# Nested attention over ragged sequences: twice as many loop bodies, V projected by tiles, and a fetch-and-jump between bodies

## The chip, the cores and the metric

The kernel runs on one core of a Trainium2 chip. The metric is the device time of one execution in microseconds (us), given as the median over several executions. Most executions of one kernel agree within a few us. Each execution carries a state, "fast" or "slow"; comparisons below use fast runs only. A ratio is the mean time of one kernel's fast runs over the mean of the other kernel's fast runs of the same rounds on the same chip, so it is not quite the ratio of the medians that are quoted beside it: the medians are over all runs, among them one slow run each of the kernel after and of e1_layout.

Names of engines in the profile: PE is TensorE's matrix multiply, PEld its weight load, DVE is VectorE, ACT is ScalarE, POOL is GpSimd, SP is SyncE. A name with q at its end (PEq) is that engine's sequencer.

## The reference, cut to what matters

```python
batch, max_seq, n_heads, head_dim = (32, 512, 8, 64)
lengths = np.random.randint(64, max_seq, size=batch)

for b in range(batch):
    seq_len = lengths[b]
    qkv = np.matmul(x[b, :seq_len], w_qkv)          # 512 -> 3 * 512
    q, k, v = ...                                    # 8 heads of 64
    scores = scale * np.matmul(q, k.transpose(0, 2, 1))
    attn = softmax(scores)                           # with 1e-08 in the denominator
    output[b, :seq_len] = np.matmul(attn, v)         # the rest stays zero
```

There are 32 sequences with lengths between 64 and 511, known only at run time.

## The kernel before

The kernel ranks the sequences by length on the chip, longest first, and takes them two at a time: 16 pairs, called pair 0 to pair 15 here. Each pair has a class, its longer length rounded up to a multiple of 32. For each class there is one body: a fixed stream of instructions for every engine, which computes the attention of two sequences and meanwhile projects Q, K and V of the next one, so that TensorE always has something to do. A tile is 128 rows, so the body of class 352 is a "three-tile" body. The bodies stand in the program one after the other, from class 512 down to 64. Each engine walks down this list; a body whose class is not the current one is jumped over, and a body whose class comes again is repeated.

```python
CLASSES = [32 * k for k in range(16, 1, -1)]

ORDER = {   # S scores, Q K V projections, A attention times V, O P stores
    4: "S S Q0 A0 S S K0 V0 S S Q1 A1 S S K1 V1 S S Q2 A2 S S K2 V2 S S Q3 A3 S S K3 V3 O",
    3: "S S Q0 A0 K0 S S V0 Q1 A1 S S K1 V1 S S Q2 A2 K2 S S V2 Q3 A3 S S K3 V3 O",
    2: "S S V0 B0 A0 b1 A1 S V1 S B2 V2 O A2 A3 b3 P V3",
}
# ... cut ...
def read_class(pr, h, N):          # once in a body, in its first half
    if h == 0:
        for g in ("pe", "act", "dve"):
            pr.add(g, lambda e: next_class(e))       # class of the next pair -> register
        k = CLASSES.index(N)
        if k + 2 < len(CLASSES):
            def hint(e):
                cur, far = regs[e.engine][1], regs["far"]
                e.reg_alu(far, cur, k + 2, ALU.is_lt)
                ahead[k + 1] = e.mark_branch_hint_location(far)
            pr.add("pe", hint)
# ... cut ...
def loops(e, name, body, pre1=None):
    r, cur = regs[e.engine]
    for k, N in enumerate(CLASSES):
        if N == P and pre1 is not None:
            pre1(e)                                  # the "bridge" to one-tile bodies
        top = nc.cur_bb
        lab, out_ = f"{name}_b{k}", f"{name}_x{k}"
        br = e.br_cmp(cur, k, lab, out_, "IS_EQ")
        if name == "pe" and k in ahead:
            br.branch_hint(ahead[k])
        nc.switch_bb(lab, parent=top)
        body(e, N)
        e.br_cmp(cur, k, lab, out_, "IS_EQ")         # the same class again?
        nc.switch_bb(out_, parent=top)
```

V is projected by pairs of heads: for each of the T tiles, four matmuls with 128 columns.

```python
def vproj(pr, bank, h, i, T):
    # ... cut: T == 1 ...
    for t in range(T):
        for c in range(NC):
            mms.append(mm(
                pa[:, bank, t * P : (t + 1) * P],
                xT[h][:, c, t * P : (t + 1) * P],
                w_r[:, c, 2 * D + i * P : 2 * D + (i + 1) * P],
                c == 0, c == NC - 1,
            ))
    group(...)
```

The softmax here doesn't subtract the row's maximum and nothing guards it: scores larger than these inputs give would overflow.

## Time and profile before

| before | value | from |
|---|---|---|
| time, median | 370.14 us (368.4 to 371.85) | 3 runs |
| span in the profile | 367.7 us | page |
| PE busy | 349.1 us, 95% | page |
| mean granted TensorE clock | 0.986 | clocks by core |
| PE gaps over 0.9 us, summed | 3.3 us | trace |

The first fence has lines of the profile's page for the kernel before. The first gives each engine's busy time; the two strips give 40 equal slices of the span, each digit the busy tenths of PE or the granted clock in tenths; the last two are the queues that the page calls "instruction": packets, megabytes and their share of the DMA engines.

```profile
PE 349.1 (95%) x4844; PEld 245.4 (67%) x4845; DVE 236.9 (64%) x537; ACT 229.2 (62%) x307; POOL 58.0 (16%) x85
...
PE   8699999999999999999999999999899999999882
...
PEclk9699999999999999999999999999999999999998
...
q8 instruction: 32, 0.52, 0.6%
q14 instruction: 22, 0.18, 0.2%
```

PE is busy nearly always: TensorE bounds this kernel, and whatever takes PE's time away shows in the time.

The view of waits (engine, line, tile, what it waited for; total us, times, longest us) has for PE and PEld in the kernel before:

```profile
PEld pa L219 <- issue: 37.3, 121, 1.3
...
PEld psc L219 <- issue: 10.2, 31, 1.0
```

"issue" means that the engine waited for nothing that the profile can see. Weight loads have such waits between groups of matmuls all the time (152 in these two lines).

### The profile page before, as it was taken

What the parts mean: (1) busy time and instruction counts of PE and PEld (TensorE: products, weight loads), DVE (VectorE), ACT (ScalarE), POOL (GpSimd) and SP (SyncE); (2) the same over time, 40 slices, a digit from 0 to 9 for tenths busy, and PEclk for the clock granted to TensorE, in tenths of its full rate; (3) what the DMA queues carried; (4) which work ended last, traced back from release to release, by engine and by line L of the source; (5) the groups of instructions that cost most, each with busy time, mean ns of one, the idle gap of its engine ahead of it and who ended that gap; (6) DMA issues with size and microseconds to landing.
All of it is one profiled execution on the core that took longest, in us unless ns stands there. A gap on an engine that the chain in (4) does not pass through costs nothing. (4 is left out here: it accounts for less than half of the span.)

```text
span 367.7 us, 12708 instructions
## 1 busy us (share of the span) xinstructions
PE 349.1 (95%) x4844; PEld 245.4 (67%) x4845; DVE 236.9 (64%) x537; ACT 229.2 (62%) x307; POOL 58.0 (16%) x85
## 2 busy tenths in 40 slices
PE   8699999999999999999999999999899999999882
PEld 3245566666656666666666677777789898887761
DVE  4455667666767667676766767676666666676562
ACT  5278778777776666666666757565566664654541
POOL 3062020202010110111011001110112112212120
PEclk9699999999999999999999999999999999999998
DMA  7969677458759677978759759969876566667673
GB/s 264 337 155 276 202 160 215 132 123 265 182 168 237 172 257 192 225 260 289 225 150 302 252 117 286 299 199 255 233 203 184 152 176 182 188 143 223 164 169 101
DMA packets 84582, 76.43 MB, mean 208 GB/s; under 512 B 42544, under 2 KB 63024, under 8 KB 84528
## 3 DMA queue, kind: packets, MB, share of 16 engines
q1 hardware_dynamic: 69376, 59.47, 59.8%
q10 hardware_dynamic: 15152, 16.26, 12.9%
q8 instruction: 32, 0.52, 0.6%
q14 instruction: 22, 0.18, 0.2%
HBM read 29.37 MB, written 36.70 MB: 180 GB/s over the span
## 5 line engine op out<-in xcount | busy, mean ns | idle before, releaser
L261 ACT ACTIVATE ep<-psc 128x704 f16<-128x704 f32 (+5 forms) x265 | 204.7, 821 | 101.3 <-PE psc L219 76.6
L219 PE MATMUL pa<-xT,w_r 128*128 128x352 f16 (+11 forms) x1056 | 161.6, 288 | 3.8 <-PEq L45 2.6
L291 DVE CAST qkT<-pa 128x352 f16<-128x352 f32 (+5 forms) x164 | 92.0, 561 | 59.5 <-PE pa L219 55.5
L219 PEld LDWEIGHTS pa<-xT,w_r 128*128 128x128 f16 x1056 | 81.4, 98 | 54.4 <-issue 27.9
L219 PE MATMUL pa<-w_r,xT 128*128 128x128 f16 (+1 forms) x1296 | 94.8, 221 | 0.1
L219 PEld LDWEIGHTS pa<-w_r,xT 128*128 128x128 f16 x1296 | 77.8, 98 | 18.4 <-issue 9.4
L324 DVE TENSOR_TENSOR v_aug<-pa,masks 128x384 f16<-128x384 f32 (+2 forms) x116 | 60.9, 525 | 31.5 <-PE pa L219 29.7
L219 PEld LDWEIGHTS pav<-v_aug,ep 128*128 128x128 f16 x1792 | 67.2, 98 | 11.7 <-ACT ep L261 3.5
L219 PE MATMUL pav<-v_aug,ep 128*128 128x65 f16 x1792 | 71.7, 194 | 2.5 <-ACT ep L261 2.4
L219 PE MATMUL psc<-qkT 64*128 64x352 f16 (+11 forms) x656 | 70.1, 299 | 1.4 <-PEq L45 0.9
L405 DVE SCALAR_TENSOR_TENSOR onat<-pav,masks,rcp 128x256 f32<-128x256 f32 (+2 forms) x128 | 51.9, 444 | 5.2 <-DVE rcp L381 0.7
L849 POOL CAST v_aug<-masks 128x24 f16 (+4 forms) x33 | 9.1, 276 | 282.1 <-POOLq L665 282.1
L844 POOL CAST x<-x_nat 128x1536 f16<-128x1536 f32 (+3 forms) x34 | 43.9, 1293 | 17.2 <-POOLq L665 16.2
L219 PEld LDWEIGHTS psc<-qkT 64*128 64x128 f16 x656 | 20.6, 94 | 21.5 <-issue 10.2
L289 ACT CAST qkT<-pa 128x448 f16<-128x448 f32 (+3 forms) x28 | 14.1, 504 | 24.4 <-ACTq L45 15.2
L381 DVE RECIPROCAL rcp<-pav 128x8 f32<-128x8 f32 (+1 forms) x68 | 14.7, 216 | 19.7 <-PE pav L219 16.0
L403 DVE TENSOR_TENSOR onat<-pav,rcp 128x512 f32<-128x512 f32 (+2 forms) x32 | 17.8, 557 | 1.1
L883 PE MATMUL psc<-zt 128*128 128x512 f16 x26 | 7.9, 468 | 1.7 <-DVE zt L905 1.7
L883 PEld LDWEIGHTS psc<-zt 128*128 128x128 f16 x26 | 2.8, 114 | 5.2 <-issue 1.9
L610 ACT ACTIVATE ep<-tiny 128x1024 f32<-128x1024 f32 x6 | 6.0, 1053 | 0.0
L790 ACT CAST w_r<-w_f 128x1024 f16<-128x1024 f32 x4 | 4.2, 1045 | 1.1 <-DMA w_f<-in_w_qkv_dram 1.1
L790 ACT ACT_TABLE_LOAD x1 | 1.3, 1283 | 3.2 <-issue 3.2
(48 smaller groups left out, 19.7 us busy)
## 6 DMA issues: line engine op xcount, KB each, us to landing
out_dram<-zt SPq DMA_DIRECT2D x16, 768.0 KB, 5.4
x_nat<-in_x_dram SPq DMA_DIRECT2D x12, 768.0 KB, 5.0
x_nat<-in_x_dram SPq DMA_DIRECT2D x8, 1024.0 KB, 6.6
out_dram<-onat ACTq DMA_DIRECT2D x28, 256.0 KB, 3.5
x_nat<-in_x_dram SPq DMA_DIRECT2D x12, 512.0 KB, 4.2
out_dram<-onat ACTq DMA_DIRECT2D x12, 384.0 KB, 3.9
out_dram<-onat SPq DMA_DIRECT2D x12, 384.0 KB, 3.6
out_dram<-zt SPq DMA_DIRECT2D x12, 256.0 KB, 4.6
```

The lines of the kernel that those rows point to most:

```text
L219: return lambda e: e.matmul(o, lhsT, rhs, start=start, stop=stop)
L261: lambda e: e.activation(out=dst, in_=src, func=AF.Exp, scale=scale),
L289: group(pr, b, eng, mms, lambda e: e.copy(out=dst, in_=src))
L291: group(pr, b, eng, mms, lambda e: e.tensor_copy(out=dst, in_=src))
L324: lambda e: e.tensor_tensor(out=v_aug[h][:, 0:T, 2 * i : 2 * i + 2, 0:HD], in0=pa[:, bank, 0 : T * P].rearrange("p (t a d) -> p t a d", a= ...
L381: pr.add("dve", lambda e: e.reciprocal(out=rv, in_=den).then_inc(s_r, 1))
L403: ins = e.tensor_tensor(op=ALU.mult, **ops)
L405: ins = e.scalar_tensor_tensor(scalar=now[0][:, 1, t : t + 1], op0=ALU.mult, op1=ALU.mult, **ops)
L610: lambda e, a=a: e.activation(out=ep32[:, i + 1, a], func=AF.Copy, in_=tiny.unsqueeze(2).broadcast_to([P, NT, MAXS // 2]),).then_inc(s_ini ...
L844: e.tensor_copy(out=x16[h][:, 0:T, :], in_=x_nat[h][:, 0:T, :]).then_inc(s_xc[h], 1)
L849: e.tensor_copy(out=v_aug[h][:, 0:T, :, HD], in_=src[:, 0, 0:T].unsqueeze(2).broadcast_to([P, T, NH]),).then_inc(s_on[h], 1)
L883: e.matmul(psc[:, 1, 0, :], zt16[:, 0:P], zt16[:, 0:MAXS], start=True, stop=True)
```

## The change

The intent has four parts. (1) A pair's second sequence may be one class (32 columns) shorter than the first, with a body of its own: 29 bodies instead of 15 (in the numbering here, 0 to 28; 24 to 28 are one-tile bodies), each of which knows how many columns it really has to project. (2) In the prologue and in bodies of three and four tiles V is projected by tiles: one group of four matmuls with 512 columns per tile instead of groups of 128 columns. Bodies of two tiles keep V by pairs of heads. (3) In the middle of its first half, each body looks up the next class, and "fetches": it compares the class with the bodies within reach and marks, for the one that fits, a hint to the later jump there. (4) At its end, the body jumps straight to the next body instead of walking down the list. The token orders of the bodies change with it. The diff, cut to its core:

```diff
+DOWN = 1
+BODIES = [(k, k + d) for k in range(NCL) for d in range(DOWN + 1) if k + d < NCL]
+REACH = 4
...
+    def vproj(pr, bank, h, t):
+        mms = []
+        for c in range(NC):
+            mms.append(
+                mm(pa[:, bank, :], xT[h][:, c, t * P : (t + 1) * P], w_r[:, c, 2 * D : 3 * D],
+                   c == 0, c == NC - 1)
...
-        3: "S S Q0 A0 K0 S S V0 Q1 A1 S S K1 V1 S S Q2 A2 K2 S S V2 Q3 A3 S S K3 V3 O",
+        3: "S S Q0 A0 K0 S S V0 Q1 A1 S S K1 V1 S S Q2 A2 V2 S S K2 A3 S S Q3 K3 O",
...
+    def targets(at):
+        end = first1 if at < first1 else len(BODIES)
+        near = [to for to in range(max(at, 0), at + REACH + 1) if to < end]
+        return sorted(near, key=lambda to: (to != at + 1, to != at + 2))
...
+    def fetch(pr, at):
+        def fn(g, e):
+            ...
+            for to in targets(at):
+                skip = to == at + 1
+                if skip and g != "pe" or g != "pe" and at < to < at + 3:
+                    continue
+                e.br_cmp(cur, number(to), f"{name}{to}", f"{name}{to}n", "IS_EQ")
+                nc.switch_bb(f"{name}{to}", parent=top)
+                if not skip:
+                    pr.ahead[g][to] = e.mark_branch_hint_location()
+                e.br(f"{name}x")
+                nc.switch_bb(f"{name}{to}n", parent=top)
+            e.br(f"{name}x")
+            nc.switch_bb(f"{name}x", parent=top)
...
-    def loops(e, name, body, pre1=None):
+    def loops(e, name, body, pre1=None, before={}):
...
+        def leave(at, ahead):
+            for to in targets(at):
+                d = f"{name}_d{at}_{to}"
+                br = e.br_cmp(cur, number(to), f"{name}_b{to}", d, "IS_EQ")
+                if to in ahead:
+                    br.branch_hint(ahead[to])
+                nc.switch_bb(d, parent=top)
+            e.br(f"{name}_x{max(targets(at))}")
+
+        leave(-1, before)
+        nc.switch_bb(f"{name}_x-1", parent=top)
+        for at in range(len(BODIES)):
+            if at == first1 and pre1 is not None:
                 pre1(e)
-            top = nc.cur_bb
-            lab, out_ = f"{name}_b{k}", f"{name}_x{k}"
-            br = e.br_cmp(cur, k, lab, out_, "IS_EQ")
-            ...
+            lab, out_ = f"{name}_b{at}", f"{name}_x{at}"
+            e.br_cmp(cur, number(at), lab, out_, "IS_EQ")
             nc.switch_bb(lab, parent=top)
-            body(e, N)
-            e.br_cmp(cur, k, lab, out_, "IS_EQ")
+            leave(at, body(e, at) or {})
             nc.switch_bb(out_, parent=top)
```

TensorE marks no hint for the next body in the list (at + 1), on the ground that it comes next anyway. And a body is now two blocks of code with the fetch's little branches between them: a head and a tail.

With the lengths of this case the bodies run in the order 1, 4, 8, 10, 10, 11, 13, 14, 16, 18, 19, 21, 22, 23, then the bridge, then 25 and 26.

## The prediction

> **What bounds the kernel now.** TensorE. The page shows PE busy 349.1 of 367.7 us, and the timeline by engine shows its groups back to back from 30.7 to 344 us. The table of busy times by stretch gives, for a pair of three-tile sequences (133 to 158 us), PE 25.1 of 25.1 us, against DVE 17.2 and ACT 16.7. Exceptions: the start (Q and K begin at 14.4 us), the prologue's end (ACT runs unpaused from 20.9 to 32 us and sets when the first pair starts), ACT's wait for the zero fill (PE lost 1.06 us at 262), ACT late at the start of short bodies (PE lost 0.46 at 321, 0.90 at 334 us), and the last six us of stores.

> **Where the change can gain.** Sorted into classes, pairs 0, 5, 6, 10, 11, 13 and 14 of the 16 have a shorter second rank; they project, and score their second half, 32 columns narrower.

> 1. Narrower columns. By the timeline a column costs 0.42 ns (four matmuls of 512: 0.87 us, of 352: 0.61). In a pair of T tiles the projections lose 64 x 32 columns = 0.85 us, scores 0.13 (T=2) to 0.5 us (T=4). Estimates: pair 0 1.4, pairs 5 and 6 1.25 each, 10 and 11 1.0 each: 5.9 us.
> 2. Pair 13 goes from 160/160 to 160/128, so its second half becomes a one-tile half. It takes 15.2 us now with the bridge (331.2 to 346.4). I estimate 6.0 (with a stall of about 1.2 us at the fence, which waits for DVE's reciprocal and products) + 3.1 + 0.8 us, so 4 to 5 us less.
> 3. Pair 14 is one-tile; there the transposes (3.2 us to landing, PE gaps of 0.27 and 1.17 us) are about as long as a half, so I expect nearly nothing.
> 4. V by tiles. 896 matmuls of 128 columns become 224 of 512. But 16 of them take 0.99 us where four of 512 take 0.87 us, and 0.08 us of this belongs to the following scores (64-row weights) and stays. So 2 to 3 ns per matmul: about 0.04 us per group of 16, 2 us in all. [...] In three-tile halves A3 now comes only one K (0.61 us) after its last scores, while ACT needs 0.75 us: perhaps 0.15 us of stall in each of 12 halves, which takes it back.
> 5. Fetch and jump. [...] ACT's "issue" gaps of 1.5 and 2.3 us at starts of bodies agree. But PE lost only about 0.5 to 1.5 us to these. More distinct bodies run (15 instead of 12), compares are hidden. Net gain about 0.5 us.
> 6. Class calculation on DVE grows about 1.1 us, absorbed while x's third tile loads.

> **Sum:** 5.9 + 4.7 + about 1 = 11.6 us: 370.1 becomes 358.5 us, range 354 to 363.5. Chances: faster 0.84, same 0.13, slower 0.03.

> **What would show it:** V matmuls at 217 ns, V's PE time nearly unchanged; pair 13 with bridge near 10 us; pairs 1 to 4, 7 to 9 within 0.3 us of before.

> **What would make it wrong:** fetch stalls at +2 to +4 jumps on ACT, DVE, SP; DVE (two-tile halves now evacuate Q3 and K3 there) becoming the limit; the A3 stalls larger; prologue's V waiting for its weights (cast ends at 22.4 us).

ACT's gaps are in the trace of the kernel before: five waits of ACT marked "issue" at starts of bodies, 1.3 to 2.3 us, 8.2 us together.

## More of the kernel before

The 32 packets of q8 have 16384 bytes each, the 22 of q14 have 8192.

Finally, a piece of PE's timeline in pair 1 (start us, length us, engine, line, operation, shapes, count):

```profile
77.31 1.06 PE L219 MATMUL pa<-w_r,xT 128*128 128x128 f16 x16
78.30 0.55 PE L219 MATMUL psc<-qkT 64*128 64x448 f16 x4
78.78 0.93 PE L219 MATMUL pa<-xT,w_r 128*128 128x448 f16 x4
79.55 1.12 PE L219 MATMUL pav<-v_aug,ep 128*128 128x65 f16 x32
```

The groups follow each other without a bracket for idle time. `pa<-w_r,xT` is a V projection, `psc` scores, `pa<-xT,w_r` a Q or K projection, `pav` attention times V.

## The result, and the profile after

| | before | after |
|---|---|---|
| median | 369.97 us (368.4 to 371.85, 4 runs) | 442.86 us (439.38 to 446.49, 4 runs, one of them slow) |
| span in the profile | 367.7 us | 440.2 us |
| PE busy | 349.1 us | 364.4 us |
| span less PE busy | 18.6 us | 75.8 us |
| mean granted clock | 0.986 | 0.911 |
| PE gaps over 0.9 us, summed | 3.3 us | 58.9 us |

The ratio is 1.194 (95% interval 1.184 to 1.204): 19% slower, where 3% faster had been predicted. The same lines of the page as before, now of the kernel after:

```profile
PE 364.4 (83%) x4080; PEld 218.2 (50%) x4081; DVE 237.4 (54%) x526; ACT 217.1 (49%) x291; POOL 57.4 (13%) x85
...
PE   7779999699779668999899589696695995978582
...
PEclk9698999899889967999999979899898899799778
...
q8 instruction: 46, 0.75, 0.7%
q14 instruction: 47, 0.39, 0.3%
```

The total loss of span splits without a rest: 57.2 us more in which PE does nothing, and 15.3 us more of PE busy, though PE now runs 4080 matmuls instead of 4844 with fewer columns. The busy time grew because the clock fell, from a mean of 0.986 to 0.911. Nor did other engines get more to do: DVE is where it was, and ACT has less. Both instruction queues brought more: 46 packets instead of 32, and 47 instead of 22.

The waits of the kernel after:

```profile
PEld pa L227 <- issue: 77.4, 148, 5.3
...
PEld psc L227 <- issue: 55.9, 81, 4.2
...
PE pa L227 <- issue: 26.2, 8, 4.9
PE psc L227 <- issue: 24.0, 9, 3.9
```

The last two lines are 17 waits of PE of the kind "issue", 50.2 us in total. In them it isn't waiting for DVE, ACT or a transfer of data, as far as the profile shows. Their place in the timeline is the first real clue. This is pair 1 again:

```profile
79.35 0.93 PE L227 MATMUL pa<-xT,w_r 128*128 128x448 f16 x4
83.86 1.03 PE L227 MATMUL pa<-w_r,xT 128*128 128x512 f16 x4 [3.58 <-issue]
```

and pairs 2, 3 and 8, and the end of pair 7:

```profile
126.47 1.89 PE L227 MATMUL pa<-w_r,xT 128*128 128x512 f16 x4 [2.56 <-issue]
...
166.79 1.46 PE L227 MATMUL pa<-w_r,xT 128*128 128x512 f16 x3 [4.93 <-issue]
...
307.55 1.04 PE L227 MATMUL psc<-qkT 64*128 64x256 f16 x8 [3.29 <-issue]
...
317.65 1.04 PE L227 MATMUL pa<-w_r,xT 128*128 128x128 f16 x8 [3.35 <-issue]
```

There are two places where PE stops. Seven times it stops in the middle of a body, each time at its fetch point (2.56 to 4.93 us, 24.8 us together: pairs 1, 2, 3, 6, 8, 9, 11). Eight times it stops at the entry of a pair, as at 307.55 us (2.11 to 3.92 us, 22.9 us together: pairs 0, 2, 3, 5, 6, 7, 8, 12). One gap of 4.23 us follows the bridge, and five of 1.1 to 1.6 us (one of them before the first projection) are of other kinds. Sum 58.9 us.

During one of those mid-body gaps, from 80.2 to 83.9 us, the view of DMA queues shows:

```profile
q1 hardware_dynamic: 896, 0.21, 41.5%
q8 instruction: 2, 0.03, 3.6%
```

Two packets of q8 start in it, the first at 80.34 us, 0.06 us after PE's last matmul ended. In each of the seven mid-body gaps a packet on q8 starts between 0.4 us before the gap and 1.8 us after its beginning, takes 0.9 to 2.3 us, and PE resumes only after it has landed. A packet alone stops nothing: 32 came on q8 in the kernel before, whose large gaps sum to 3.3 us, and none of the 32 starts inside one of these gaps.

The clock's part shows in the table of busy times by stretch (stretch, length, then busy us of PE, PEld, DVE, ACT, POOL, then the granted clock, the DMA share and GB/s), just after the entry gap of pair 2 and the mid-body gap of the same pair:

```profile
116.00:119.40 3.40, 3.21 (x27) 1.86 (x28) 0.56 (x1) 1.51 (x2) 1.76 (x2) 0.50 0.35 116
126.30:129.70 3.40, 3.23 (x11) 0.88 (x12) 0.75 (x1) 0.86 (x2) 0.00 (x0) 0.50 1.02 378
129.70:133.00 3.30, 3.30 (x41) 1.69 (x40) 1.51 (x3) 1.77 (x3) 0.00 (x0) 1.00 0.32 122
```

After most of the gaps, PE runs for 3.4 to 10.2 us at half clock (granted 0.50), so that such a gap costs more than its own length: the four matmuls at 126.47 us took 1.89 us, the same group at 83.86 us, still at full clock, 1.03 us. The kernel after has 15 half-clock stretches, the kernel before has 2, one near the start and one at the end. Of the 16 gaps over 2 us in the list above, 13 came with a half-clock stretch; those of pairs 5, 6 and 12 (2.11, 2.46 and 3.05 us at the entry) did not, so the length of a gap alone does not tell. The gaps of 2.56 and 2.60 us of pair 2 came with 3.4 us at 0.50 each, the one of 3.05 us with none.

### Where the code stands

The compiled instruction stream of TensorE explains the places. It was read from the built program (no view of the profile shows it), with the number of the first and last matmul slot of each part of a body:

```
kernel after, TensorE
body  1:  head 1092 to 1294   tail 1309 to 1945
body  4:  tail 3686 to 4322   head 4331 to 4533
body  8:  tail 6986 to 7414   head 7423 to 7561
body 10:  tail 8166 to 8594   head 8603 to 8741
```

Bodies 0 to 3 stand as they were written. From body 4 on, up to the last two-tile body, the blocks were laid out with the tail before its own head. The cause in the source is the chain of fall-back labels x0, x1, ...: `leave` ends with a jump to x{max(targets)}, a label that earlier bodies so refer to, and the layout of blocks puts x{at-1} and the head after it behind the tail. (That the labels are the cause is shown by the first experiment below, which does away with them and gets the written order.) So with its own fetch point each such body jumps back, to its tail: by about 850 instructions in body 4, 575 in bodies 8 and 10, 465 in most two-tile bodies and 280 in the last one; and from the end of the tail it jumps over its own head and over the next tail to the next head. "The next body needs no hint, it comes next anyway" was no longer true.

At each of the fifteen gaps of the two kinds a packet of 16384 bytes on q8 starts between 0.5 us before the gap and 1.8 us after its beginning. (That q8 is TensorE's is inferred: PE resumed in the mid-body gaps only after such a packet had landed, and the runs e8_pefetch and e9_allhint, which change the fetch of ACT and DVE alone, moved q14, from the 47 packets of e6_align to 44 and 49, and left q8 at 40. Which engines q14 serves, the trace does not say.) A part that ran again did not always bring packets: body 10 ran a second time in pair 4, and no packet on q8 starts after 163.69 us and before 214.12 us, at that pair's end. The stall was 2.1 to 4.9 us, the transfer of the packet itself 0.9 to 2.3 us.

The pattern of the mid-body gaps fits this layout to the last body. All seven rotated bodies that were entered by a jump of +2 or more (4, 8, 10, 13, 16, 18, 21) stopped in their middle. Of the six passes that began by a jump of +1 or in the same body (10 again, 11, 14, 19, 22, 23), none did: there the tail had just run or lies just behind what ran before; why PE did not stop there is not shown. Three of those five +1 entries (11, 14, 22) stopped at the entry instead (2.11, 3.92 and 3.05 us), where the head lies behind the tail and no hint was given. The entries with a hint are not explained: the trace has nine hint records of TensorE, for the entries of pairs 0 to 4, 6, 8, 9 and 11, and those of pairs 0, 2, 3, 6 and 8 stopped all the same.

### The profile page after: what moved, and what is told of

Same layout as the page of the kernel before. It is cut to its first block, busy times and chain, and to the rows that moved or that the text cites. A ratio compares the mean times of both kernels' runs of the same rounds, so it can differ in the third digit from the quotient of the medians.

```text
span 440.2 us, 11342 instructions
## 1 busy us (share of the span) xinstructions
PE 364.4 (83%) x4080; PEld 218.2 (50%) x4081; DVE 237.4 (54%) x526; ACT 217.1 (49%) x291; POOL 57.4 (13%) x85
## 5 line engine op out<-in xcount | busy, mean ns | idle before, releaser
L269 ACT ACTIVATE ep<-psc 128x704 f16<-128x704 f32 (+6 forms) x261 | 197.7, 807 | 193.8 <-PE psc L227 157.9
L227 PE MATMUL pa<-xT,w_r 128*128 128x96 f16 (+12 forms) x1056 | 159.6, 294 | 8.4 <-PEq L51 6.0
L299 DVE CAST qkT<-pa 128x352 f16<-128x352 f32 (+6 forms) x172 | 93.6, 549 | 74.7 <-PE pa L227 73.1
L227 PE MATMUL pa<-w_r,xT 128*128 128x128 f16 (+1 forms) x568 | 97.0, 311 | 26.7 <-issue 24.7
L227 PE MATMUL psc<-qkT 64*128 64x352 f16 (+12 forms) x644 | 69.8, 310 | 25.2 <-issue 24.0
L227 PE MATMUL pav<-v_aug,ep 128*128 128x65 f16 x1768 | 76.2, 200 | 4.6 <-issue 1.6
L227 PEld LDWEIGHTS pav<-v_aug,ep 128*128 128x128 f16 x1768 | 70.7, 102 | 17.6 <-issue 7.0
L311 DVE TENSOR_SCALAR v_aug<-pa,masks 128x512 f16<-128x512 f32 x62 | 46.6, 752 | 60.3 <-PE pa L227 55.5
L227 PEld LDWEIGHTS pa<-w_r,xT 128*128 128x128 f16 x568 | 43.0, 105 | 59.3 <-issue 39.4
L902 POOL CAST x<-x_nat 128x1536 f16<-128x1536 f32 (+3 forms) x34 | 43.1, 1268 | 15.6 <-POOLq L720 15.1
L334 DVE TENSOR_TENSOR v_aug<-pa,masks 128x256 f16<-128x256 f32 x40 | 16.9, 422 | 24.2 <-PE pa L227 24.0
L391 DVE RECIPROCAL rcp<-pav 128x8 f32<-128x8 f32 (+1 forms) x67 | 14.4, 215 | 24.4 <-PE pav L227 19.5
L297 ACT CAST qkT<-pa 128x384 f16<-128x384 f32 (+3 forms) x16 | 8.0, 500 | 15.9 <-ACTq L51 12.4
```

The costliest lines, as they stand in the source:

```text
L227: return lambda e: e.matmul(o, lhsT, rhs, start=start, stop=stop)
L269: lambda e: e.activation(out=dst, in_=src, func=AF.Exp, scale=scale),
L297: group(pr, b, eng, mms, lambda e: e.copy(out=dst, in_=src))
L299: group(pr, b, eng, mms, lambda e: e.tensor_copy(out=dst, in_=src))
L311: lambda e: e.tensor_scalar(out=v_aug[h][:, t, :, 0:HD], in0=pa[:, bank].rearrange("p (h d) -> p h d", d=HD), scalar1=now[0][:, 0, t : t + ...
L334: lambda e: e.tensor_tensor(out=v_aug[h][:, 0:T, 2 * i : 2 * i + 2, 0:HD], in0=pa[:, bank, 0 : T * P].rearrange("p (t a d) -> p t a d", a= ...
```

## The experiments

The theory: most of the loss is the place of the code, heads behind tails, and what jumps over them cost; the computation that the change wanted is nearly as good as predicted. The rivals: the fetch point costs by itself (its compares, the hints); V by tiles and the new order leave PE short of ready work; more bodies and narrower columns need other bodies more often, wherever they stand. Nine kernels ran; all gave the right result. The kernel before ran in the same rounds with medians of 370.57 us (e1 to e4), 370.48 us (e5 to e7) and 369.48 us (e8, e9).

All spans and gaps below are from the profiled run:

| run | median us | ratio to before, 95% interval | span | PE busy | clock | PE gaps over 0.9 us |
|---|---|---|---|---|---|---|
| after | 442.86 | 1.194 (1.184 to 1.204) | 440.2 | 364.4 | 0.911 | 58.9 |
| e1_layout | 383.13 | 1.037 (1.032 to 1.043) | 378.2 | 345.5 | 0.970 | 17.4 |
| e2_nofetch | 402.08 | 1.084 (1.082 to 1.087) | 403.3 | 352.7 | 0.940 | 36.6 |
| e3_vtiles | 372.10 | 1.004 (1.002 to 1.006) | 370.7 | 350.7 | 0.981 | 4.0 |
| e4_down0 | 371.87 | 1.002 (0.998 to 1.006) | 371.3 | 350.2 | 0.983 | 7.5 |
| e5_down0_rot | 395.80 | 1.065 (1.059 to 1.071) | 395.7 | 360.2 | 0.957 | 23.2 |
| e6_align | 367.32 | 0.991 (0.986 to 0.997) | 365.9 | 339.6 | 0.982 | 9.3 |
| e7_best | 367.34 | 0.989 (0.983 to 0.995) | 366.1 | 338.8 | 0.983 | 10.5 |
| e8_pefetch | 367.67 | 0.994 (0.988 to 1.000) | 365.1 | 340.1 | 0.981 | 7.5 |
| e9_allhint | 369.48 | 0.998 (0.990 to 1.005) | 368.1 | 338.7 | 0.988 | 11.1 |

### e1_layout: the same bodies, head directly before tail

The fall-back labels between bodies are replaced by one block before the one-tile bodies and one at the end. In the kernel after, the entry checks at these labels were run only on the fall-back path, so all but a few of the executed instructions are the same: the same 4080 matmuls in the same order.

```diff
-        def leave(at, ahead):
+        def leave(at, ahead, tos=None, other=None):
-            for to in targets(at):
+            for to in tos or targets(at):
...
-            e.br(f"{name}_x{max(targets(at))}")
+            e.br(other or f"{name}_{'one' if at < first1 else 'end'}")
...
-            if at == first1 and pre1 is not None:
-                pre1(e)
-            lab, out_ = f"{name}_b{at}", f"{name}_x{at}"
-            e.br_cmp(cur, number(at), lab, out_, "IS_EQ")
-            nc.switch_bb(lab, parent=top)
+            if at == first1:
+                nc.switch_bb(f"{name}_one", parent=top)
+                if pre1 is not None:
+                    pre1(e)
+                leave("one", {}, list(range(first1, len(BODIES))), f"{name}_end")
+            nc.switch_bb(f"{name}_b{at}", parent=top)
             leave(at, body(e, at) or {})
```

> The kernel after, with the same blocks and the same instructions in them, but the entry checks and skip labels between bodies removed, so that the toolchain lays the blocks out as written: each body's first part (up to the fetch) directly before its second part. In the kernel after, from the fifth body on, the second part lies before the first, so PE jumps some 650 to 850 instructions back in the middle of a body. Theory 'placement': the 7 gaps in the middle of bodies (24.7 us of PE waiting on issue) go, and the gaps at the entry of the bodies that follow directly (pairs 5, 7, 12: 9.1 us) go; some of those after jumps over a body stay; with the clock restored I expect 370 to 388 us. Rival 'fetch code': the compares, taken branches and hints themselves, or twice the code, cost the time wherever they lie: 425 us or more. Rival 'order of the work': V by tiles and the new orders cost it: no change, about 442 us.

Measured: 383.13 us, 60 us less than after. In the built program every tail follows its head. Pair 1's timeline at the place where the kernel after stopped for 3.58 us, and the waits:

```profile
78.08 0.93 PE L227 MATMUL pa<-xT,w_r 128*128 128x448 f16 x4
78.91 1.03 PE L227 MATMUL pa<-w_r,xT 128*128 128x512 f16 x4
```

```profile
PEld pa L227 <- issue: 37.5, 113, 2.8
PEld psc L227 <- issue: 35.6, 78, 4.1
...
PE psc L227 <- issue: 7.0, 2, 3.9
```

None of the seven mid-body gaps is left. Against after, the span fell by 62.0 us: 43.1 us of idle PE and 18.9 us of PE busy, which is the clock (0.911 to 0.970). That is 86% of the whole loss of 72.5 us. By the medians the fall is 59.7 us; the profiled run of e1_layout was its fastest. So the place of the code is the main cause, shown by changing almost nothing else. (The edit moves the blocks of every engine, since all use the same `loops`; that the stops were TensorE's own is read from its waits and branch records.) It isn't the whole: the kernel is still 3.7% slower than before, with 17.4 us of large gaps, among them 3.13 us after the prologue, 3.87 us at the entry of pair 11 and 2.68 us early in pair 14.

### e2_nofetch: good places, but no fetch point

As e1_layout, and `fetch` does nothing:

```diff
-        pr.ahead = {}
+        pr.ahead = {g: {} for g in ("pe", "act", "dve")}
+        return
```

> As e1_layout, and the fetch (compares and branch hints inside the bodies) taken out on all engines; only the jumps at the ends stay. If hints help: PE stalls about 3.5 us at each of some 9 jumps over a body, so 10 to 25 us slower than e1_layout (390 to 405 us). If the fetch code itself is the cost: faster than e1_layout.

Measured: 402.08 us, 19 us more than e1_layout. PE stops at the entry of eight of the 14 pairs before the bridge, for 2.3 to 5.5 us each, which is this line of its waits:

```profile
PE psc L227 <- issue: 29.0, 8, 5.5
```

So the fetch point is not the cost; with heads and tails in order it saves 19 us by the medians. (The profiled spans, 403.3 against 378.2 us, differ by 25 us, but they are of the slowest run of e2_nofetch and the fastest of e1_layout.) The rival "the fetch costs by itself" is out.

### e3_vtiles: the kernel before, with V by tiles and the new orders

```diff
+        if T >= 3:
+            for c in range(NC):
+                mms.append(
+                    mm(pa[:, bank, :], xT[h][:, c, i * P : (i + 1) * P], w_r[:, c, 2 * D : 3 * D],
+                       c == 0, c == NC - 1)
+                )
+            group(...)
+            return
...
-        3: "S S Q0 A0 K0 S S V0 Q1 A1 S S K1 V1 S S Q2 A2 K2 S S V2 Q3 A3 S S K3 V3 O",
+        3: "S S Q0 A0 K0 S S V0 Q1 A1 S S K1 V1 S S Q2 A2 V2 S S K2 A3 S S Q3 K3 O",
```

(the four-tile order and the prologue's order changed likewise)

> The kernel before with only V by tiles (three and four tiles), and the orders of work for them and for the prologue, from the kernel after. My prediction: V itself gains 2 us, the third A's stall takes some back: 368 to 371 us. Rival 'order of the work' (this part is what made the kernel after slow): over 400 us.

Measured: 372.1 us, ratio 1.004. Three-tile pairs without a class change take 25.83 to 25.93 us instead of 25.62 to 25.66: 0.2 to 0.3 us more each. V by tiles is next to neutral, a little worse, and cannot explain 72 us. The forecast, 368 to 371 us, was missed by 1 us. The profiled run also has a stop that isn't V's, at the entry of pair 2, where the list jumps over a class. The timeline of PE there:

```profile
107.07 0.60 PE L219 MATMUL psc<-qkT 64*128 64x384 f16 x4 [2.38 <-issue]
```

### e4_down0: good places, one body for each class again

As e1_layout with `DOWN = 0`: no shorter second rank, 15 bodies.

```diff
-DOWN = 1
+DOWN = 0
```

> As e1_layout with DOWN = 0: one body per class, both ranks of a pair at the first one's class, so no narrower projections. Against e1_layout this takes out the gain that I estimated at 10 to 11 us from narrower columns and pair 13, and takes out half of the bodies, so fewer jumps over a body (4 instead of 9, at about 2.5 us each). Expected 372 to 385 us; if narrowing gains what I said and jumps cost what I said, within 5 us of e1_layout.

Measured: 371.87 us, ratio 1.002. With the bodies in order, fetch and jump over 15 bodies is as good as the list of before, no better: the prediction's gain of 0.5 us for it is within the noise. The second half of the expectation, within 5 us of e1_layout, was missed: e1_layout took 11 us more in the same rounds. So the third rival is true in part: even in good places, 29 bodies at first cost more in jumps than their narrower columns gained (large PE gaps of 17.4 us in e1_layout, 7.5 in e4_down0).

### e5_down0_rot: the kernel after with one body for each class

The kernel after with `DOWN = 0` alone, so its tails stand before their heads. Against e4_down0, only the placement differs.

> The kernel after with DOWN = 0 and nothing else: one body per class, as e4_down0, but with the jump labels of the kernel after, so that from the fifth body on the second part again lies before the first. If placement is the cause, this is slow with the old number of bodies too: 8 bodies (pairs 2, 3, 6 to 11 and 12) run for the first time in that form, each with about 3.5 us in its middle and 2 to 3.5 us at its entry, and the clock lost after it: 415 to 440 us. If the doubled code is needed for the loss: within 10 us of e4_down0 (371.9 us).

Measured: 395.8 us, 24 us more than e4_down0 (in other rounds; the ratios to before are 1.065 and 1.002): the placement costs without any change of the work. The size was a miss: 415 to 440 us had been expected. Here is the same place of pair 2 in e5_down0_rot, and then in e4_down0:

```profile
110.00 0.82 PE L227 MATMUL pa<-xT,w_r 128*128 128x384 f16 x4
113.23 1.04 PE L227 MATMUL pa<-w_r,xT 128*128 128x512 f16 x2 [2.41 <-issue]
```

```profile
110.34 0.82 PE L227 MATMUL pa<-xT,w_r 128*128 128x384 f16 x4
111.00 1.03 PE L227 MATMUL pa<-w_r,xT 128*128 128x512 f16 x4
```

This is the only mid-body gap in e5_down0_rot. The others are five entry gaps of 2.25 to 3.41 us (pairs 3, 6, 7, 8, 9). With 15 bodies only one rotated body is entered by a jump of more than one, body 4 in pair 2, and this is the one that stops in its middle; the five entry gaps are all jumps of +1 (two more, into pairs 11 and 12, did not stop). For the gap inside a body it is the pattern of the kernel after, and it fits that fewer bodies lost less: with twice the bodies, seven of the 13 jumps between pairs 0 and 13 became +2 or more, and many bodies stopped at their entry and in their middle.

### e6_align: e1_layout, with heads placed at fixed offsets

This kernel pads TensorE's stream so that heads start 64 instructions (three and four tiles), 0 (others) or 100 (the last two-tile body) after a multiple of 256, aligns the prologue as well, and gives the bodies after the bridge hints from the last two-tile body.

```diff
+    HEAD = [64 if CLASSES[k] > 2 * P else 0 for k, _ in BODIES]
+    HEAD[first1 - 1] = 100
...
+            tos = targets(at)
+            if at == first1 - 1 and g == "pe":
+                tos = tos + list(range(first1, len(BODIES)))
...
+        pr.add("pe", lambda e: e.addr_align(256, offset=176, max_nops=0))
...
+            if name == "pe" and nxt < len(BODIES) and at != first1 - 1:
+                e.addr_align(256, offset=(HEAD[nxt] - 1) % 256, max_nops=0)
```

> As e1_layout, and on PE alone: padding that is never run puts the head of each body at a fixed place[...], the prologue is moved[...], and the chain of compares after the bridge gets hints. Theory: the remaining gaps of e1_layout at jumps (3.1 us after the prologue, 2.3 into pair 2, 3.9 into pair 11, 0.8 + 2.7 in pair 14) come from hinted blocks fetched too late[...]. Then they shrink by 8 to 12 us together, and with the clock: 366 to 374 us. If hints don't work that way: within 3 us of e1_layout (383 us).

Measured: 367.32 us, ratio 0.991 (0.986 to 0.997): faster than before, by a little under 1%. The gap after the prologue fell from 3.13 to 0.97 us, and pair 14, the first after the bridge, from 10.75 to 7.60 us. The entry of pair 11, first in e1_layout, then in e6_align:

```profile
309.62 0.82 PE L227 MATMUL pa<-xT,w_r 128*128 128x192 f16 x8
314.31 0.70 PE L227 MATMUL psc<-qkT 64*128 64x192 f16 x8 [3.87 <-issue]
```

```profile
304.42 0.82 PE L227 MATMUL pa<-xT,w_r 128*128 128x192 f16 x8
305.17 0.51 PE L227 MATMUL psc<-qkT 64*128 64x192 f16 x8
```

Three things changed together and the offsets were chosen for this path of bodies, so which of them did this is not shown, nor a rule for when a hint helps. One large gap stayed, 2.31 us at the beginning of pair 2, the jump from body 4 to body 8. The timelines of ACT, DVE and PE have there:

```profile
107.84 2.92 ACT L269 ACTIVATE ep<-psc 128x768 f16<-128x768 f32 x4 [3.80 <-issue]
...
107.96 1.02 DVE L299 CAST qkT<-pa 128x384 f16<-128x384 f32 x2 [3.19 <-issue]
...
108.71 0.34 PE L227 MATMUL psc<-qkT 64*128 64x384 f16 x2 [2.31 <-ACT ep L269]
```

PE waits for ACT here, and ACT and DVE wait for nothing visible, right after their jump. With TensorE mended, other engines' jumps come to light.

### e7_best: e6_align, with V by pairs of heads in three-tile bodies

```diff
-        3: "S S Q0 A0 K0 S S V0 Q1 A1 S S K1 V1 S S Q2 A2 V2 S S K2 A3 S S Q3 K3 O",
+        3: "S S Q0 A0 K0 S S W0 Q1 A1 S S K1 W1 S S Q2 A2 K2 S S W2 Q3 A3 S S K3 W3 O",
```

(W is V by pairs of heads; three-tile heads then start at offset 0)

> As e6_align, with V of three-tile halves by pairs of heads in the order of the kernel before (T2 tiles). The traces of e1_layout and e3_vtiles show three-tile pairs at 25.8 to 25.9 us against 25.6 before, so 0.2 to 0.35 us per pair come back: 1 to 2 us less than e6_align; 364 to 372 us, and perhaps faster than the kernel before (370.6).

Measured: 367.34 us, ratio 0.989. Pairs 3 to 7 take 0.1 to 0.5 us less than in e6_align, pair 2 takes 1.7 us less and pair 8 takes 3.1 us more in the profiled run, so the whole is not to be told from e6_align. The intervals of both lie just below 1.

### e8_pefetch and e9_allhint: ACT's and DVE's own fetch

Both are e6_align with TensorE's part untouched. e8_pefetch takes the fetch point from ACT and DVE; e9_allhint lets them mark hints for +2 and for the same body as well.

```diff
 e8:
-        for g in ("pe", "act", "dve"):
-            pr.add(g, lambda e, g=g: fn(g, e))
+        pr.ahead = {g: {} for g in ("act", "dve")}
+        pr.add("pe", lambda e: fn("pe", e))
 e9:
-                if skip and g != "pe" or g != "pe" and at < to < at + 3:
+                if skip and g != "pe":
```

> Same as e6_align, but ACT and DVE have no fetch point in the middle of a body any more (no compares, no hints); only TensorE keeps it. In e6_align TensorE still loses 2.3 us at the first two bodies of pair 2, because ACT is idle for 3.80 us and DVE for 3.19 us marked issue at that +4 jump although both had fetched. Theory A (ACT's and DVE's fetch helps the +3 and +4 jumps, only not enough at pair 2): without it pairs 1, 2, 3 and 10 lose 0.5 to 3 us each, 369 to 374 us. Theory B (the fetch on ACT and DVE [...] is the reason of the 3.8 us): the gap in pair 2 shrinks to below 1 us, 364 to 366 us. Matmul stream unchanged in both.

> Same as e6_align, but ACT and DVE also fetch ahead for a jump of +2 and for staying in the same body (before: only for +3 and +4). Theory A (a hint that is missing costs something at +2 jumps): small gaps at entries of pairs 3, 5, 10 to 12 that ACT ends shrink by 0.2 to 1 us each, 364 to 367 us; the +4 jump of pair 2 stays at 2.3 us. Theory B[...]: nothing or a shift of a gap from one pair to another, 366 to 370 us.

Measured: 367.67 and 369.48 us; the intervals of both overlap that of e6_align and include 1. Without its fetch, ACT's gap at pair 2 shrank from 3.80 to 2.32 us and pair 2 from 31.29 to 29.79 us; no other pair grew by more than 0.3 us (the prologue, by 0.7 us). So the fetch on ACT and DVE brings nothing measurable here, and part of the stall at pair 2 comes with it (theory B of e8, but only in part: PE still stops there twice, 0.83 and 1.44 us). With hints for +2, pair 1 became 1.6 us longer, with a new gap of ACT of 2.44 us, and none of the pairs named (3, 5, 10 to 12) got shorter: as theory B of e9 expected (366 to 370 us), for a reason that is not shown. What would clear pair 2 fully stays open.

## Why the prediction was wrong

The prediction was 358.5 us (354 to 363.5); the measured time was 442.86 us. The step that failed is item 5, "More distinct bodies run (15 instead of 12), compares are hidden. Net gain about 0.5 us". It was costed by the number of compares and by stalls that ACT had shown before. Where the compiler would put the two halves of each body was not asked; the prediction took the order of the source for the order in memory. What the runs showed in its place:

- The placement cost 62.0 us of span in the profiled runs (after against e1_layout; 59.7 us by the medians): 43.1 us of idle PE and 18.9 us through the lower clock. The second term was not in the prediction at all.
- With the placement mended, something that e6_align removed still cost about 12 us: e1_layout to e6_align, 378.2 to 365.9 us of span (15.8 us by the medians, in different rounds). It shows at jumps of TensorE: the gap after the prologue fell from 3.13 to 0.97 us, the entry of pair 11 from 3.87 us to none, and pair 14 after the bridge took 7.60 us instead of 10.75; since e6_align changed three things at once, the share of each is not shown.
- Of what could make it wrong, the prediction named "fetch stalls at +2 to +4 jumps on ACT, DVE, SP". It had a stall, but the wrong engines and only the jumps between bodies: the stalls were TensorE's own, and about half of them lay inside a body, at the jump from head to tail that the written order does not have. ACT and DVE show one in e6_align, pair 2, of 2.3 us for PE.

The other items can be read where the placement doesn't hide them, from a body's first scores to the next body's:

| item | predicted gain | measured |
|---|---|---|
| 1 narrower columns, pairs 0, 5, 6, 10, 11 | 5.9 us | 3.6 us: 1.2, 1.0, 0.7, 1.1, and -0.4 in pair 11 (e4_down0 to e6_align) |
| 2 pair 13 with the bridge | 4 to 5 us (15.2 to about 10) | 2.9 us (15.2 in before, 12.3 in e6_align) |
| 3 pair 14 | nearly nothing | 0.5 us longer than before (e6_align) |
| 4 V by tiles | a wash | 0.2 to 0.3 us lost per three-tile pair (e3_vtiles) |
| 5 fetch and jump | 0.5 us | in before's set of bodies 0 (e4_down0); in the kernel after a loss of about 60 us by the placement alone |

Item 1 was right in mechanism; its sizes for pairs 6 and 11 were too high. Item 2's stall at the fence was predicted as about 1.2 us and measured as 1.27 us; but the bridge grew by 0.5 us (0.73 to 1.23), and pair 13 without the bridge took 11.1 us where 6.0 + 3.1 = 9.1 us had been estimated. Pair 2 is the item that was missing from the sum: 27.16 us before, 31.29 in e6_align. The order of tokens is not the reason: e4_down0 has the same order, jumps by two bodies there, and takes 26.84 us. (The 28.42 us of e3_vtiles include its stop of 2.38 us.) That leaves the jump from body 4 to body 8, at which ACT and DVE stand still (3.80 and 3.19 us). Pair by pair, from before to e6_align, the sum is -1.8 us, of which pair 13 without the bridge gives -3.4, pair 0 -1.7, pairs 5, 6 and 10 together -2.1, and pair 2 takes back 4.1.

Item 4 had also named V's duration: the group of four 512-column matmuls takes 1.03 us in the listings above (they start 215 to 217 ns apart, as predicted), the 16 of 128 columns 1.06 us (mostly 56 ns apart, in the kernel before). That was right, and so was the lack of a gain.

## What to carry to other kernels

When a kernel has many bodies and jumps between them, read the compiled order of its blocks before anything else: labels that are referred to from earlier code can turn a body inside out, and here a part that was not laid out in the order of execution cost 2 to 5 us wherever TensorE stopped for it, and in 12 of 15 cases some us at half clock beside it. In the profile, look for PE waits marked "issue" of over 2 us with a packet on the instruction queue beside them; they belong to no data and no engine as far as the profile shows, and an average of busy time doesn't name them. A prefetch by hint was worth having here (19 us), but with a layout in which what is not hinted really comes next; in the rotated layout five of nine hinted entries stopped all the same.
